# One encoder layer in float32 on one core: block stores and gate rows on GpSimd's queue, and the modulation's row sums behind the addition of each matrix' second bank

## The chip, the core and the metric

The kernel runs on one core of a Trainium2 chip. Its engines work side by side: TensorE multiplies matrices (PE, with weight loads as PEld), VectorE (DVE) and ScalarE (ACT) work element by element, GpSimd (POOL) and SyncE (SP) here do little but issue DMAs. Each engine runs its own instructions in order and waits on the others by semaphores. The metric is the device time of one execution, in microseconds (us).

## The reference, cut to what matters

```
h = x + 0.5 * g1 * postRMS(SwiGLU_1(mod1(preRMS(x))))      # FFN 1
h = h + g2 * postRMS(Mixer(mod2(preRMS(h))))               # two kinds of attention
h = h + 0.5 * g3 * postRMS(SwiGLU_2(mod3(preRMS(h))))      # FFN 2
swiglu(u, w_gate, w_up, w_down) = (silu(u @ w_gate) * (u @ w_up)) @ w_down
```

x is 1024 x 1024 in float32, D_FF is 2816. The shifts, scales and gates (mod1 to mod3, g1 to g3) are 9 columns of 1024 numbers: silu(c) times a 1024 x 9216 matrix, plus a bias.

## The kernel before, in words

Every product is computed as three float32r products of high and low halves, hence two operands "H" and "L" of everything (tiles wsH/wsL for weights) and three matmuls per 128 x 128 by 128 x 512 block, on lines 307 to 309.

The gate and up products of an FFN, the stage this is about, run over 11 pairs (NPAIR) of one gate and one up matrix, each a column block of 256 of the weights. An object `Matrix` forms its product by a Strassen-like scheme with seven block products of 12 matmuls instead of eight. TensorE's order within a matrix is: A11 and A12 times the input's first half (`start`), then `p6` (operand T2), `p5` (T1), `p7` (T3), `p3` (B22) and `p4` (T4); a pair is 168 matmuls. The products p7 and p4 pile up in one bank of PSUM with the former ones. After p7 VectorE adds this bank to the tile c22: that is `self.added`, L419. p4's first matmul writes into the same bank and so waits until L419 has read it. p3's addition is L424, and the first product's is L389.

The sums of weight blocks that the scheme needs (S1 to S4) come from two loads, raw (L325) and raw2 (L337) of 512 KB, and are four VectorE additions into two tiles s21 and s34: L340, L341, L351, L352. They are cast to H by ScalarE and to L by VectorE (L350, L232). A pair's two results give the hidden block silu(gate) x up; `hidden` (L488 to L491) forms its sums s21 and s34, and stores three blocks hd_A of 256 KB (L494) and two d_S of 512 KB to DRAM. `down_sums` does the like for the down weights (t21 and t34, L515 to L518) and stores two d_T of 512 KB. `both` issues the d_S and d_T stores on L505; `store_queue(c)` gives their queue, SP for all pairs but the last, POOL (GpSimd) for that. All of the tiles s21, s34, t21, t34 share one tag "s" of four buffers: a new sum waits until the store that reads the old tile has landed.

The modulation's columns are made beside all this. A row of the matrix (512 KB, tile wada) is loaded by SP, and one VectorE instruction multiplies it by silu(c) and sums it (`mod_sum`, L79: a custom instruction over 128 x 1024 and a read of its accumulator). 32 such row sums are steps of a generator in FFN 1 (eight for the gate g1, sixteen for mod2, eight for g2) and eight in FFN 2 (g3); `per_pair` says how many steps are taken after which pair: in FFN 1 none before pair 3, five after pairs 3 to 8, four after pair 9; in FFN 2 two from pair 2 on. A finished gate of eight columns goes to DRAM as a row (`g_dram`, L121), to be read back across all partitions.

The order of instructions on each engine is not written out: a scheduler takes the program's order, dependences and its own estimates, and moves an instruction ahead of others where its inputs are ready. `tc.issue_after(ins)` keeps what is issued in its block behind `ins`, on the same engine; no semaphore is added by it there. DMA issue is in the order of each queue.

Of the kernel before, what the change touches and what calls it, by code (L numbers as in the profile page):

```python
# [20 lines left out]
P = 128  # L21
D = 1024
S = 1024
NK = D // P
# [9 lines left out]
NPAIR = NFF // 2  # L34
# [12 lines left out]
def build(ctx, tc, A, out):  # L47
    nc = tc.nc
    V, ACT, PE, POOL, SP = nc.vector, nc.scalar, nc.tensor, nc.gpsimd, nc.sync
# [31 lines left out]
    def mod_col(mp, j, c, add, scale=None):  # L81

        t = const.tile([P, NK], F32, name=f"modcol{j}")
        for k in range(NK):
            w = mp.tile([P, D], F32, name="wada", tag="row", bufs=ROWS - 1)
            SP.dma_start(w, A["wada"][j * NK + k])
            mod_sum(w, c, t[:, k:k + 1], add[:, k:k + 1], 1.0 if scale is None else scale[:, k:k + 1])
            yield
        return t
# [4 lines left out]
    def post_cols(i):  # L94
        return badaT[:, (3 * i + 2) * NK:(3 * i + 3) * NK], npostT[:, i * NK:(i + 1) * NK]
# [21 lines left out]
    def mod_gate(mp, i, c):  # L117

        g = yield from mod_col(mp, 3 * i + 2, c, *post_cols(i))
        row = dram.tile([1, D], F32, name=f"g_dram{i}")  # L120
        SP.dma_start(row.rearrange("o (k p) -> p (o k)", p=P), g)  # L121
        gates[i] = row.broadcast_to([P, D])

    ab, gates = {}, {}
# [186 lines left out]
    class Matrix:  # L311
# [80 lines left out]
        second = "pb", 1  # L392
# [10 lines left out]
        def start(self):  # L403
            self.part(8)
# [30 lines left out]
    def rest(late, m, between=None):  # L435

        m.sums(late, False)
        m.sums34()
        m.last()
        if between is not None:  # L440
            between()
        m.p6()
        m.p5()
        m.p7()
        m.p3()
        m.p4()

    def rest_first(late, ms, done):

        for m in ms[:2]:
            m.p6()
        for i, m in enumerate(ms[:2]):
            m.p5()
            m.last()
            if i:
                ms[2].sums(late, True)
            m.p3()
            m.p7()  # L460
        for m in ms[:2]:
            m.p4()
        ms[2].sums34()
        ms[2].last()
        for i in range(2, len(ms)):
            m, nxt = ms[i], ms[i + 1] if i + 1 < len(ms) else None
            m.p6()
            done(i - 1)
            m.p5()
            m.p7()  # L470
            if nxt is not None:
                with tc.issue_after(m.copied.ins), tc.issue_after(m.added.ins):
                    nxt.sums(late, True)
            m.p3()
            if nxt is not None:
                nxt.sums34()
            m.p4()
            if nxt is not None:
                nxt.last()
        done(len(ms) - 1)  # L480

    def hidden(late, c, hs, hd):


        a11, a12, a21, a22 = hs["C11"], hs["C21"], hs["C12"], hs["C22"]
        s21 = late.tile([P, 2, HALF], F32, name="s21", tag="s", bufs=4)
        s34 = late.tile([P, 2, HALF], F32, name="s34", tag="s", bufs=4)
        V.tensor_add(s21[:, 1], a21, a22)  # L488
        V.tensor_sub(s21[:, 0], s21[:, 1], a11)
        V.tensor_sub(s34[:, 0], a11, a21)  # L490
        V.tensor_sub(s34[:, 1], a12, s21[:, 0])  # L491
        for n, t in (("A11", a11), ("A12", a12), ("A22", a22)):
            hd[n, c] = dram.tile([P, HALF], F32, name=f"hd_{n}_{c}_{len(hd)}")
            store_queue(c).dma_start(hd[n, c], t)  # L494
        both(hd, "S2", "S1", c, s21)
        both(hd, "S3", "S4", c, s34)

    def store_queue(c):

        return POOL if c == NPAIR - 1 else SP  # L500

    def both(hd, n0, n1, c, t):
        d = dram.tile([P, 2, HALF], F32, name=f"d_{n0}_{c}")
        hd[n0, c], hd[n1, c] = d[:, 0], d[:, 1]
        store_queue(c).dma_start(d, t)  # L505

    def down_sums(fp, late, src, c, hd):

        r1 = wpool.tile([P, 2, HALF], F32, name="raw", tag="raw", bufs=2)
        SP.dma_start(r1, src[:, 0:2])  # L510
        r2 = fp.tile([P, 2, HALF], F32, name="raw2", tag="raw2", bufs=2)
        SP.dma_start(r2, src[:, 2:4])
        t21 = late.tile([P, 2, HALF], F32, name="t21", tag="s", bufs=4)
        t34 = late.tile([P, 2, HALF], F32, name="t34", tag="s", bufs=4)
        V.tensor_sub(t21[:, 1], r1[:, 1], r1[:, 0])  # L515
        V.tensor_sub(t21[:, 0], r2[:, 1], t21[:, 1])
        V.tensor_sub(t34[:, 0], r2[:, 1], r1[:, 1])
        V.tensor_sub(t34[:, 1], r2[:, 0], t21[:, 0])  # L518
        both(hd, "T2", "T1", c, t21)
        both(hd, "T3", "T4", c, t34)  # L520

    def ffn(wg, wu, wd, start, pending, steps_fn, per_pair, steps2_fn, i, res_src, dst):


        hd = {}

        with tc.tile_pool(name="ffa", bufs=1, side="left", reuse_waits="tile") as fp, \
                tc.tile_pool(name="ffa_ps", bufs=1, space=PSUM, reuse_waits="tile") as psum:
            mats = {}

            def pair(c):
                g = Matrix(fp, psum, A[wg][c], None)
                mats[c] = g, Matrix(fp, psum, A[wu][c], g)
                return mats[c]

            first = [m for c in range(NFIRST) for m in pair(c)]
            start(fp, psum, first)
            with tc.tile_pool(name="fft", bufs=1, side="left", reuse_waits="tile") as tp, ExitStack() as more:
                pools = [tp]
                later = pending(pools, fp, psum, tag="y")  # L540
                for n, m in enumerate(first):
                    m.start()
                    if n:
                        next(later)
                with tc.tile_pool(name="ffs", bufs=1, side="left", reuse_waits="tile") as sp:
                    for m in first[:2]:
                        m.sums(sp, True, "s0")
                    for m in first[:2]:
                        m.sums34()
                pools.append(more.enter_context(tc.tile_pool(name="fft2", bufs=1, side="left", reuse_waits="tile")))  # L550
                for _ in later:
                    pass
                yp.close()
                with tc.tile_pool(name="late", bufs=1, side="right", reuse_waits="tile") as late:
                    steps = steps_fn(late)
                    def follow(n):
                        if n % 2 and n // 2 < NFIRST - 1:
                            hidden(late, n // 2, mats[n // 2][1].c, hd)
                        if n > 1:

                            if n % 2 == 0:
                                down_sums(fp, late, A[wd][n // 2 - 1], n // 2 - 1, hd)
                            for _ in range((per_pair(n // 2) + n % 2) // 2):
                                next(steps, None)

                    rest_first(late, first, follow)
                    for c in range(NFIRST, NPAIR):
                        for second, m in enumerate(pair(c)):
                            if second:
                                down_sums(fp, late, A[wd][c], c, hd)  # L570
                            m.start()

                            def between(m=m, c=c):
                                with tc.issue_after(m.summed.ins):
                                    hidden(late, c - 1, mats[c - 1][1].c, hd)
                                    if c == NFIRST + 1:
                                        down_sums(fp, late, A[wd][NFIRST - 1], NFIRST - 1, hd)

                            rest(late, m, None if second else between)
                        for _ in range(per_pair(c)):  # L580
                            next(steps, None)
                    hidden(late, NPAIR - 1, mats[NPAIR - 1][1].c, hd)
                    for _ in steps:
                        pass

        open_y()
        with tc.tile_pool(name="ffb0", bufs=1, side="left", reuse_waits="tile") as np_, \
# [9 lines left out]
            steps = steps2_fn(np_)  # L597
# [4 lines left out]
            def raw(n, c, cols=slice(0, HALF)):  # L602
                t = fp.tile([P, HALF], F32, name="stg", tag="stg", bufs=STG)[:, cols]
                loads.append(SP.dma_start(t, (A[wd][c][:, B[n]] if n in B else hd[n, c])[:, cols]))
                return t
# [57 lines left out]
            for p, (sn, tn, bk) in enumerate((("A11", "B11", "A"), ("A12", "B21", "B"), ("S2", "T2", "A"), ("S1", "T1", "B"),  # L663
# [8 lines left out]
                if p < 6:  # L672
                    for c in range(NPAIR):
# [5 lines left out]
                        with ahead:  # L679
                            s, t = halves(fp, raw(sn, c), "sb", SB), halves(fp, raw(tn, c), "tb", NPAIR)  # L680
# [820 lines left out]
```

## Time and the profile before

| | us |
|---|---|
| median of three runs | 2202.57 |
| the three runs | 2201.4, 2202.57, 2205.51 |
| the profiled execution | 2207.76 |
| its span | 2206.0 |
| TensorE busy | 2141.8 |
| VectorE busy | 1555.9 |
| ScalarE busy | 1050.0 |
| GpSimd busy | 58.4 |

The granted clock of TensorE was 0.994 of full speed over the span. FFN 1's gate and up products run from about 0 to 476 us, those of FFN 2 from about 1560 to 1980 us. In a row of the profile, "L419 TENSOR_TENSOR q<-bank,q 128x512" is an instruction of line 419 that writes tile q from tiles bank and q; "SPq" and "POOLq" are the DMA issues of the two queues; a bracket such as "[1.42 <-DVE q L419]" is how long the engine had been idle before, and what released it.

### The profile page before, as it was taken

Reading aid. Unit: us, or ns where it says so; the run is one execution under the profiler, and the core shown is the slowest. Engines: PE = TensorE matmul, PEld = TensorE weight load, DVE = VectorE, ACT = ScalarE, POOL = GpSimd, SP = SyncE. Lnnn points to the kernel's source line nnn. Section 1 sums busy time; section 2 is a strip of 40 time slices with the busy share of each in tenths; the row PEclk is TensorE's granted clock in tenths of the full one; section 3 lists DMA queues with packets and bytes.
Section 4 is the critical chain, followed back from the end, with each engine's and each line's share of the span. In section 5 each row is a group of like instructions: output and inputs, shape, how many; then the busy total and the mean of one; then the engine's idle time right before and its main releaser. Section 6 shows DMA issues by size and latency. Waiting matters only on the chain.

```text
span 2206.0 us, 28418 instructions
## 1 busy us (share of the span) xinstructions
PE 2141.8 (97%) x10328; PEld 1773.2 (80%) x10328; DVE 1555.9 (71%) x2629; ACT 1050.0 (48%) x1876; POOL 58.4 (3%) x84
## 2 busy tenths in 40 slices
PE   6899999999999999999999999999999999999997
PEld 4677788878887877888888988788788888888886
DVE  7989766658677678576677576665987767655566
ACT  6633333335465556455455455565733333334453
POOL 0000000000000010001011000000000000000000
PEclk9999999999999999999999999999999999999999
DMA  8488744359785111110212122763475644437675
GB/s 330 139 280 305 212 148 176 134 188 332 255 273 167 41 46 46 34 56 27 70 56 65 37 89 95 253 199 127 150 234 197 220 146 157 159 126 256 196 243 182
DMA packets 139791, 355.50 MB, mean 161 GB/s; under 512 B 19457, under 2 KB 29313, under 8 KB 139650
## 3 DMA queue, kind: packets, MB, share of 16 engines
q1 hardware_dynamic: 138018, 347.91, 46.5%
q0 software_dynamic: 1632, 5.77, 0.7%
q8 instruction: 81, 1.33, 0.2%
q14 instruction: 60, 0.49, 0.1%
HBM read 265.00 MB, written 88.62 MB: 160 GB/s over the span
## 4 chain that ended last, share of the span: by engine, by line
PE 76%; DVE 12%; DMA 6%; ACT 3%; issue 2%; SPq 0%; DVEq 0%; ACTq 0%
PE bank L307 10%; PE bank L308 10%; PE bank L309 10%; PE bankB L611 7%; PE bankA L611 7%; PE pps L940 5%; PE pps L942 5%; PE pps L944 5%; DMA stg<-d_T 2%; DVE f L1146 1%; PE vps L940 1%; PE vps L944 1%; PE vps L942 1%; PE pav L1157 1%; PE ops L193 1%
## 5 line engine op out<-in xcount | busy, mean ns | idle before, releaser
L940 PE MATMUL pps<-uH,wsH 128*128 128x512 f32 x512 | 209.7, 410 | 0.0
L942 PE MATMUL pps<-uL,wsH 128*128 128x512 f32 x512 | 204.8, 400 | 0.0
L944 PE MATMUL pps<-uH,wsL 128*128 128x512 f32 x512 | 203.5, 397 | 0.0
L232 DVE TENSOR_TENSOR tbL<-stg,tbH 128x512 fp32r<-128x512 f32 x154 | 106.0, 690 | 104.3 <-ACT tbH L231 103.9
L231 ACT CAST tbH<-stg 128x512 fp32r<-128x512 f32 x154 | 95.6, 621 | 148.1 <-DMA stg<-d_T 106.3
L307 PE MATMUL bank<-uH,wsH 128*128 128x512 f32 x352 | 138.4, 399 | 4.1 <-DVE q L389 1.6
L611 PE MATMUL bankA<-tbL,sbH 128*128 128x512 f32 x352 | 138.4, 393 | 3.8 <-DVE tbL L232 3.7
L308 PE MATMUL bank<-uL,wsH 128*128 128x512 f32 x352 | 139.4, 396 | 1.6 <-DVE uL L847 1.5
L309 PE MATMUL bank<-uH,wsL 128*128 128x512 f32 x352 | 139.0, 395 | 1.5 <-DVE wsL L232 1.5
L611 PE MATMUL bankA<-tbH,sbH 128*128 128x512 f32 x352 | 135.3, 394 | 4.8 <-DVE q L371 1.7
L611 PE MATMUL bankA<-tbH,sbL 128*128 128x512 f32 x352 | 137.4, 391 | 0.9 <-DVE sbL L232 0.9
L134 DVE TENSOR_TENSOR wsL<-raw,wsH 128x1024 fp32r<-128x1024 f32 x72 | 88.0, 1222 | 63.8 <-ACT wsH L134 59.4
L232 DVE TENSOR_TENSOR sbL<-stg,sbH 128x512 fp32r<-128x512 f32 (+1 forms) x176 | 108.2, 620 | 23.5 <-ACT sbH L231 22.7
L231 ACT CAST wsH<-raw 128x1024 fp32r<-128x1024 f32 (+1 forms) x88 | 73.5, 835 | 103.7 <-PE bank L308 85.1
L231 ACT CAST sbH<-stg 128x512 fp32r<-128x512 f32 (+1 forms) x176 | 98.2, 565 | 50.2 <-DMA stg<-hd_A 34.0
L944 PEld LDWEIGHTS pps<-uH,wsL 128*128 128x128 f32 x512 | 96.9, 189 | 17.8
L940 PEld LDWEIGHTS pps<-uH,wsH 128*128 128x128 f32 x512 | 97.7, 191 | 14.9
L942 PEld LDWEIGHTS pps<-uL,wsH 128*128 128x128 f32 x512 | 97.3, 190 | 14.3
L134 ACT CAST wsH<-raw 128x1024 fp32r<-128x1024 f32 x72 | 75.2, 1049 | 65.4 <-PE pps L942 36.5
L611 PE MATMUL bankB<-tbH,sbH 128*128 128x512 f32 x264 | 102.7, 389 | 0.0
L611 PE MATMUL bankB<-tbL,sbH 128*128 128x512 f32 x264 | 102.7, 389 | 0.0
L611 PE MATMUL bankB<-tbH,sbL 128*128 128x512 f32 x264 | 102.7, 389 | 0.0
(252 smaller groups left out, 5812.9 us busy)
## 6 DMA issues: line engine op xcount, KB each, us to landing
wada<-in_wada SPq DMA_DIRECT2D x56, 512.0 KB, 5.5
raw<-in_wg SPq DMA_DIRECT2D x50, 512.0 KB, 7.0
raw<-in_wu SPq DMA_DIRECT2D x50, 512.0 KB, 4.7
raw<-in_wd SPq DMA_DIRECT2D x44, 512.0 KB, 4.4
stg<-d_S SPq DMA_DIRECT2D x88, 256.0 KB, 3.7
stg<-d_T SPq DMA_DIRECT2D x88, 256.0 KB, 3.9
d_S<-s SPq DMA_DIRECT2D x40, 512.0 KB, 5.3
d_T<-t SPq DMA_DIRECT2D x40, 512.0 KB, 5.3
```

The lines of the kernel that those rows point to most:

```text
L134: made[:] = ACT.copy(h, raw).ins, eng.tensor_sub(l, raw, h.bitcast(F32)).ins
L193: PE.matmul(ps, aH, bL, start=False, stop=False)
L231: ACT.copy(h, src)
L232: eng.tensor_sub(l, src, h.bitcast(F32))
L307: PE.matmul(ps, H[:, ks], bH, start=first and k == 0, stop=False, skip_group_check=not first)
L308: PE.matmul(ps, H[:, ks], bL, start=False, stop=False, skip_group_check=not first)
L309: PE.matmul(ps, L[:, ks], bH, start=False, stop=k == 3, skip_group_check=not first)
L611: PE.matmul(ps, a[:, ts], b, start=first and n == 0, stop=last and n == 2, skip_group_check=not check)
L940: PE.matmul(ps, aH, bH, start=i == 0, stop=False)
L942: PE.matmul(ps, aH, bL, start=False, stop=False)
L944: PE.matmul(ps, aL, bH, start=False, stop=i == n - 1)
L1146: V.tensor_tensor_scan(fr, fr, fr, 1.0, ALU.mult, ALU.bypass)
```

## The change

```diff
@@ mod_gate
         row = dram.tile([1, D], F32, name=f"g_dram{i}")
-        SP.dma_start(row.rearrange("o (k p) -> p (o k)", p=P), g)
+        dst = row.rearrange("o (k p) -> p (o k)", p=P)
+        for k in range(0, NK, 4):
+            POOL.dma_start(dst[:, k:k + 4], g[:, k:k + 4])
         gates[i] = row.broadcast_to([P, D])
@@ hidden
-            store_queue(c).dma_start(hd[n, c], t)
+            POOL.dma_start(hd[n, c], t)
@@ both
-        store_queue(c).dma_start(d, t)
+        POOL.dma_start(d, t)
@@ ffn, in the loops over pairs and over a pair's two matrices
                             rest(late, m, None if second else between)
-                        for _ in range(per_pair(c)):
-                            next(steps, None)
+                            with tc.issue_after(m.added.ins):
+                                for _ in range((per_pair(c) + second) // 2):
+                                    next(steps, None)
```

(`store_queue` is deleted.) All block stores and the gate rows, each of these now two DMAs of four columns, are issued by GpSimd. The steps of the row sums, until now after a pair, come behind the addition `added` of each matrix: of five, two behind the gate matrix and three behind the up matrix. In FFN 1 that is in pairs 3 to 8, and two more behind each matrix of pair 9 as far as steps are left; in FFN 2, behind one matrix each, in pairs 3 to 5. Lines from L121 on stand two later in the changed program up to `hidden`, L505 is L503, and L515 to L518 are L513 to L516: L419 is now L421, and L340, L341, L351, L352 are L342, L343, L353, L354.

What this does to the order of VectorE's instructions in the steady part of FFN 2, first before. The row L419 is the addition of a gate matrix; s_17110 and s_17111 are the sums of the up matrix of its pair, s_17238 and s_17239 those of the next pair's gate matrix (whose tiles were t21 and t34 before).

```order
L340 TENSOR_TENSOR s_17110<-raw_17108 128x512
L341 TENSOR_TENSOR s_17110<-s_17110,raw 128x512
L351 TENSOR_TENSOR s_17111<-raw,raw_17108 128x512
L352 TENSOR_TENSOR s_17111<-raw,s_17110 128x512
L350 TENSOR_TENSOR wsL<-s_17110,wsH 128x512 x2
L419 TENSOR_TENSOR q<-bank,q 128x512
L340 TENSOR_TENSOR s_17238<-raw_17236 128x512
L351 TENSOR_TENSOR s_17239<-raw,raw_17236 128x512
L341 TENSOR_TENSOR s_17238<-s_17238,raw 128x512
L424 TENSOR_TENSOR q<-bank_17001,q 128x512
```

The same place in the changed program:

```order
L342 TENSOR_TENSOR s_17113<-raw_17111 128x512
L353 TENSOR_TENSOR s_17114<-raw,raw_17111 128x512
L343 TENSOR_TENSOR s_17113<-s_17113,raw 128x512
L354 TENSOR_TENSOR s_17114<-raw,s_17113 128x512
L342 TENSOR_TENSOR s_17241<-raw_17239 128x512
L353 TENSOR_TENSOR s_17242<-raw,raw_17239 128x512
L352 TENSOR_TENSOR wsL<-s_17113,wsH 128x512
L343 TENSOR_TENSOR s_17241<-s_17241,raw 128x512
L352 TENSOR_TENSOR wsL<-s_17113,wsH 128x512
L354 TENSOR_TENSOR s_17242<-raw,s_17241 128x512
L421 TENSOR_TENSOR q<-bank,q 128x512
L426 TENSOR_TENSOR q<-bank_17004,q 128x512
```

The four sums of the next pair's gate matrix stood behind the addition and now stand ahead of it, so the addition also waits for what they wait for. This is so at six gate matrices of FFN 2 (pairs 3 and 5 to 9) and at one of FFN 1 (pair 3).

VectorE in FFN 1, before, at the end of the blocks' sums of an early pair: s_1202 and s_1203 are sums of a hidden block, the L79 rows are row sums of the modulation, and L419 is the addition of the matrix then at work.

```order
L489 TENSOR_TENSOR s_1202<-s_1202,q 128x512
L79 ISA wada,modcol_2000<-wada,csil,colsT 128x1024
L79 ISA modcol_2000 128x1
L491 TENSOR_TENSOR s_1203<-q,s_1202 128x512
L79 ISA wada,modcol_2000<-wada,csil,colsT 128x1024
L79 ISA modcol_2000 128x1
L79 ISA wada,modcol_2000<-wada,csil,colsT 128x1024
L79 ISA modcol_2000 128x1
L419 TENSOR_TENSOR q<-bank,q 128x512
```

In the changed program, at the addition of the up matrix of FFN 1's pair 3 (L373 are the products of the up matrix' results with the gate's):

```order
L421 TENSOR_TENSOR q<-bank,q 128x512
L79 ISA wada,modcol_1530<-wada,csil,colsT 128x1024
L79 ISA modcol_1530 128x1
L373 TENSOR_TENSOR q<-q 128x512
L79 ISA wada,modcol_1530<-wada,csil,colsT 128x1024
L79 ISA modcol_1530 128x1
L426 TENSOR_TENSOR q<-bank_1623,q 128x512
L79 ISA wada,modcol_1530<-wada,csil,colsT 128x1024
L79 ISA modcol_1530 128x1
```

The row sums that stood ahead of the addition stand behind it, and with them between it and the next results.

GpSimd's queue, nearly empty before, in FFN 1 around the second half of a gate row (hd_A, d_S and d_T are the stores of hidden block and down weights, 48 to 50 and the like are numbers of blocks):

```order
L496 DMA hd_A_4_48_2072<-q 128x512
L123 DMA g_dram_1998<-modcol_1530 128x4x1
L496 DMA hd_A_4_50_2076<-q 128x512
L496 DMA hd_A_4_49_2074<-q 128x512
L503 DMA d_S_4_2078<-s_2066 128x1024
L503 DMA d_S_4_2080<-s_2067 128x1024
L503 DMA d_T_5_2169<-t_2163 128x1024
L503 DMA d_T_5_2171<-t_2164 128x1024
```

The stores of a pair now follow one another on this queue with the half rows among them. SP's queue, which had them all between the loads of weights, keeps the loads alone.

More of the change, by code (lines that the diff above doesn't have):

```diff
@@ L493, in hidden @@
             hd[n, c] = dram.tile([P, HALF], F32, name=f"hd_{n}_{c}_{len(hd)}")
-            store_queue(c).dma_start(hd[n, c], t)
+            POOL.dma_start(hd[n, c], t)
         both(hd, "S2", "S1", c, s21)
         both(hd, "S3", "S4", c, s34)
-    def store_queue(c):
-        return POOL if c == NPAIR - 1 else SP
     def both(hd, n0, n1, c, t):
```

## The prediction

> **What bounds the kernel now.** I read the page's head, the busy line and the chain first, then the stretches of the two gate/up stages, then the waits inside the one that is not full.
>
> ```profile
> span 2206.0 us, 28418 instructions
> PE 2141.8 (97%) x10328; PEld 1773.2 (80%) x10328; DVE 1555.9 (71%) x2629; ACT 1050.0 (48%) x1876; POOL 58.4 (3%) x84
> PE 76%; DVE 12%; DMA 6%; ACT 3%; issue 2%; SPq 0%; DVEq 0%; ACTq 0%
> ```
>
> TensorE is busy for 97% of the span, and the matmuls are not touched by the change: the number of them stays, and their order but for one swap. So the change can only take away or add time in which TensorE stands, and only in the gate and up products of the two FFNs, where its instructions are. Next the stretches (columns: window, its length, then busy time and count of PE, PEld, DVE, ACT and POOL, the granted clock, the DMA engines' share, GB/s):
>
> ```profile
> 120.00:150.00 30.00, 28.17 (x122) 22.30 (x121) 26.45 (x42) 9.63 (x15) 0.00 (x0) 1.00 0.75 263
> 150.00:180.00 30.00, 29.84 (x131) 24.05 (x129) 29.00 (x46) 12.88 (x19) 0.00 (x0) 1.00 0.90 321
> 180.00:210.00 30.00, 28.46 (x124) 22.92 (x123) 28.31 (x44) 9.95 (x16) 0.00 (x0) 1.00 0.83 276
> 210.00:240.00 30.00, 29.47 (x129) 23.75 (x129) 26.31 (x41) 10.53 (x16) 0.00 (x0) 1.00 0.87 313
> 240.00:270.00 30.00, 29.36 (x130) 23.83 (x129) 23.43 (x36) 9.79 (x16) 0.00 (x0) 1.00 0.76 178
> 270.00:300.00 30.00, 30.00 (x134) 24.86 (x133) 20.90 (x31) 10.65 (x17) 0.00 (x0) 1.00 0.52 183
> 1800.00:1830.00 30.00, 30.00 (x134) 24.86 (x133) 17.29 (x25) 10.49 (x16) 0.00 (x0) 1.00 0.31 112
> ```
>
> A full stretch holds 134 matmuls in 30 us (0.224 us each), at full clock. From 120 to 270 us, in FFN1, there are 636 where five full stretches would hold 670: 34 x 0.224 = **7.6 us lost**; by busy time 145.3 of 150, so 4.7 us, since a matmul's modelled end hides a part of each gap. From 270 us on, and in FFN2, the stage is full: nothing is to be won there, only lost. The waits of the weight loads in 120 to 270 us say at what TensorE stood, and the T4 group's row how much of that was idle time:
>
> ```profile
> PEld bank L307 <- DVE q L419: 5.7, 5, 1.8
> PEld bank L309 <- DVE wsL L350: 1.4, 2, 0.9
> PEld bank L309 <- DVE wsL L232: 1.0, 1, 1.0
> L307 PE MATMUL bank<-T4H,wsH 128*128 128x512 f32 x36 | 14.6, 406 | 3.5 <-DVE q L419 3.4
> ```
>
> The most costly is the first matmul of the seventh block product (T4). It writes over the bank that L419 must have read first, so it stands whenever VectorE comes late to L419. Why it is late is in VectorE's rows:
>
> ```profile
> L79 DVE CUSTOM_DVE_ANT_0 wada<-wada,csil,colsT 128x1024 f32<-128x1024 f32 x32 | 41.8, 1324 | 8.8 <-DMA wada<-in_wada 8.8
> ...
> 203.60 1.34 DVE L79 CUSTOM_DVE_ANT_0 wada<-wada,csil,colsT 128x1024 f32<-128x1024 f32 x1 [1.69 <-DMA wada<-in_wada]
> 204.87 0.68 DVE L419 TENSOR_TENSOR q<-bank,q 128x512 f32<-128x512 f32 x1
> ...
> 205.61 0.50 PE L307 MATMUL bank<-T4H,wsH 128*128 128x512 f32 x1 [1.42 <-DVE q L419]
> ```
>
> All 32 row sums of FFN1's modulation stand between 90 and 260 us, 1.32 us each, and VectorE is busy for 23 to 29 of each 30 us there against 21 after it. Here one sum waits 1.69 us for its row, runs 1.34, and only then L419 runs; 0.74 us after L419's start T4 goes. The last of the five stalls has another cause, a store that lands late:
>
> ```profile
> 261.71 0.69 DVE L351 TENSOR_TENSOR s<-raw,raw 128x512 f32<-128x512 f32 x1 [1.06 <-DMA d_S<-s]
> ...
> 264.87 0.50 PE L307 MATMUL bank<-T4H,wsH 128*128 128x512 f32 x1 [0.64 <-DVE q L419]
> ```
>
> **Term 1: the row sums go behind the addition.** The 32 sums move from 90 to 260 us into slots of two behind the gate matrix' addition and three behind the up matrix', in pairs 3 to 8, and two in pair 9. No sum can then stand ahead of the L419 of its own matrix, and the load is spread over six pairs of 38 us. VectorE has 30.00 - 20.90 = 9.1 us idle in 30 us without sums, 11.5 in a pair of 168 matmuls, 38 us; five sums are 5 x 1.32 = 6.6 us of it. Four of the five T4 stalls stand behind a sum: 3.4 us of idle time less the 0.64 at 264.87 is 2.8, say 3 us as the least gain. The most is all 7.6. The waits at wsL (L350, L232) are mostly VectorE running behind after such a stall, so they go with it, but a weight that comes late by itself stays. I take **-6.5 us**, near the upper end since the whole deficit lies in the stretch where the sums are.
>
> **Term 2: what stands behind the sums in FFN1.** Three sums behind the up matrix' addition are 3 x 1.32 = 4.0 us of VectorE time, into which the third product's addition and the hidden blocks' sums are queued; the d_S stores issue after those, and the next sums wait for these stores' landing. About 1.3 us of that time was idle, so this chain is 2.6 us later. At 261.71 the same wait has shown its price, 1.06 us with 0.64 us of it on TensorE. Six gate matrices can be so affected: 0 to 1.1 each, 0 to +7 in all. I take 0.3 each, **+2 us**, by the row at 264.87 halved, since the stores also no longer wait in SP's queue.
>
> **Term 3: the stores on GpSimd's queue, and the order that VectorE gets by it.** This is the term that I think decides. In the steady pair of before:
>
> ```profile
> 330.32 0.69 DVE L518 TENSOR_TENSOR t<-raw,t 128x512 f32<-128x512 f32 x1
> 338.64 0.69 DVE L419 TENSOR_TENSOR q<-bank,q 128x512 f32<-128x512 f32 x1 [0.55 <-PE bank L309]
> 339.43 0.69 DVE L340 TENSOR_TENSOR s<-raw 128x512 f32<-128x512 f32 x1
> 340.04 0.69 DVE L351 TENSOR_TENSOR s<-raw,raw 128x512 f32<-128x512 f32 x1
> ...
> 330.31 1.04 SPq L505 DMA_DIRECT2D d_T<-t  x2
> 332.44 1.13 SPq L337 DMA_DIRECT2D raw<-in_wg  x1
> ...
> 341.16 0.39 PE L307 MATMUL bank<-T4H,wsH 128*128 128x512 f32 x1
> ```
>
> L419 ends at 339.33, and only behind it come the next gate's sums (L340, L351), which need two things: the s tiles, free when the two d_T stores have landed, and the tile raw2, loaded at 332.44. T4 wants to start at 341.16, so L419 has until 341.16 - 0.74 = 340.4. In the changed order four sums of the next gate stand *ahead* of L419 (L421 there) at seven gates: six in FFN2 (pairs 3 and 5 to 9) and one in FFN1 (pair 3). From the start of the sum that needs the second d_T store to L421 are some five instructions at 0.6 us (339.43 to 340.04), 3.0 us; so that store must have landed by 340.4 - 3.0 = 337.4. VectorE ends the t tiles at 330.32 + 0.69 = 331.0; with half an issue of GpSimd's 0.62 us (1.25 for two, below) the store is out at 331.3, so it has **6.05 us from issue to landing**. The rows on that:
>
> ```profile
> 444.84 1.25 POOL L505 DMA_DIRECT2D d_T<-t  x2 [443.53 <-DVE t L516]
> ...
> d_T<-t POOLq DMA_DIRECT2D x2, 512.0 KB, 4.9
> ...
> d_T<-t POOLq DMA_DIRECT2D x2, 512.0 KB, 6.3
> stg<-hd_A SPq DMA_DIRECT2D x1, 256.0 KB, 6.3
> ...
> d_T<-t SPq DMA_DIRECT2D x2, 512.0 KB, 5.3
> raw<-in_wg SPq DMA_DIRECT2D x2, 512.0 KB, 6.9
> ```
>
> The first is how GpSimd issues a pair; the next two are its landings at 440 to 450 and 1943 to 1952 us, with 256 KB of another load beside the second; the last two are SP's at 326 to 333 us. On one queue the stores go first and the gate's loads behind them (6.9 us). With stores on a second queue the two loads, 1 MB, run beside them. Were the rate shared evenly, I estimate from 4.9 us with little beside and 6.3 with a quarter of that beside, some 7.2 us at the worst: 1.15 us late. The same holds for raw2, which landed at about 332.44 + 6.9 = 339.3 and is now wanted by about 337. Against that, the loads no longer wait for the stores' issue. So 0 to 1.1 us for each of the six gates of FFN2, 0 to +6.6, where nothing is to be won. I take 0.3 each, **+2 us**: the landing of 6.3 us is 0.25 late. The cover is the 0.25 to 1.2 us between a landing of 4.9 and of 6.05; with it gone, each further microsecond costs one per gate.
>
> The Trainium skill has a rule on this, in "DMA: Bandwidth & Descriptors", section "Issuing engines are not separate DMA queues": transfers started by different engines run on the same 16 DMA engines and interleave, and a second issuing engine saves only the time of issuing. The trace agrees as far as it goes (4.9 us alone, 6.3 beside a load). By that rule alone the stores' move would win nothing and this term would be its upper half.
>
> The issue itself costs nothing: POOL is busy 58.4 us of 2206, and 0.6 us an issue for some 150 stores hides behind its idle time; SP's queue is 0% of the chain, so taking them off it gains nothing there either.
>
> **Term 4: the gate row** goes from one DMA to two of four columns, behind the sums on GpSimd's queue, where hidden stores stand next to them.
>
> ```profile
> g_dram<-modcol SPq DMA_DIRECT2D x3, 4.0 KB, 9.7
> ...
> 121.00:131.00 10.00, 10.00 (x46) 8.29 (x45) 9.06 (x15) 5.11 (x9) 0.00 (x0) 1.00 0.35 27
> 132.00:142.00 10.00, 8.17 (x33) 5.78 (x33) 8.40 (x14) 2.07 (x3) 0.00 (x0) 1.00 1.02 416
> ```
>
> For ten microseconds after such a row's issue the DMA engines move 27 GB/s, and at once after it 416, when TensorE stands. Two halves should hold the transfers up for about 5 us each, estimated by halving 9.7, at a place between pairs' stores. A store held up so costs up to 3 us (that landing 5 us later, less the 1 to 2 us of slack above); none, if it falls where no store is due. I take **0** (0 to +3), since a stall of this kind, in before, is already in the 7.6.
>
> **The sum**: -6.5 + 2 + 2 + 0 = -2.5 us. The profiled execution took 2207.76 us for its span of 2206.0, so 2205.3 by it; it is 5.2 us above the median of the runs, 2202.57, and from that median I get **2200 us**. A measurement of this kernel tells some 0.2%, or 4.4 us, from no change.
>
> **The rivals.** *Faster*: the stores land in time everywhere, so terms 2 and 3 are nothing, and term 1 comes whole or with more: -6.5 to -7.6, 2195 to 2196. For it: POOL's landing of 4.9, and the loads that are issued earlier. Against it: the DMA engines at 400 GB/s in the steady pair. *Slower*: the store's landing passes 6.05 us, since the loads of the next gate interleave with it; at 7.2 the seven gates lose 1.15 us each, 8, the six others of FFN1 1 us each by term 2, 6, less 6.5: +7.5, 2210. Its place is L421 behind the four sums, and the point from which it decides against the gain is a mean lateness above 0.5 us at 13 gates. Against it: SP's own 5.3. *The stores' move does nothing and only the sums count*, the order being harmless: -4 to -6.5, 2196 to 2198.5; on the border of the first. *The change doesn't do what it says*: the sums could still reach ahead of an addition, that of the following matrix; 2 behind the gate's and 3 behind the up's are 2.6 and 4.0 us, and matrices are 19 us apart, so hardly.
>
> By the skill's section "Queues, rings and completion order" of the same page each DMA engine goes round between the queues that have work, a packet at a time; that is the even sharing of the slower rival, and no row here shows it alone at this place.
>
> **How the numbers follow.** My forecast, within 0.2%: 0.38. Faster by more (the first rival, and the better half of the third): 0.36. Slower: 0.26. The likeliest case' own range is 2198.2 to 2207. For 8 in 10 I take 2195 (term 1 at 7.6 with nothing given back) to 2210 (the slower rival's price), and leave the ends beyond to both sides, since several of the latenesses would have to come together for more.
>
> **What would show it.** Term 1: no T4 wait for L421 behind L79 in FFN1, and 134 matmuls in each 30 us from 120 to 240. Term 2: waits of sums for d_S at gate matrices 4 to 9 of FFN1. Term 3: in FFN2, waits of L342 or L353 for d_T or raw2 and, behind them, of T4 for L421 at six gates; landings of d_T on GpSimd's queue under or over 6.05 us tell the rivals apart. Term 4: no stretch of 27 GB/s longer than 6 us. I am wrong if VectorE's order on the chip has the waits elsewhere, above all if hidden stores queue behind a gate row on GpSimd.

## The result, and the profile after

The changed kernel took 2271.3 us (median of six runs, 2262.08 to 2276.92) where the kernel before took 2207.1 beside it: the ratio is 1.0286, 95% interval 1.027 to 1.0302. It is slower by some 63 us, far outside the range of the prediction. The page of the profiled execution (span, busy time of each engine, and the row of the first T4 matmuls):

```profile
span 2262.3 us, 28547 instructions
PE 2156.2 (95%) x10328; PEld 1780.7 (79%) x10328; DVE 1553.1 (69%) x2629; ACT 1047.9 (46%) x1876; POOL 140.5 (6%) x230
L309 PE MATMUL bank<-T4H,wsH 128*128 128x512 f32 x176 | 73.2, 416 | 33.7 <-DVE q L421 33.7
```

VectorE and ScalarE are busy as before. The span is 56 us longer, and TensorE's account of it has three parts: it stands 33.7 us ahead of the first T4 matmul, where it stood 3.5 before; it stands 11.9 us in four waits for a copy by ScalarE (at 265.29, 433.37, 1755.18 and 1840.82); and with the same 10328 matmuls it is busy 14.4 us longer, 2156.2 in place of 2141.8. The stretches, with the columns of before (two of FFN 2 at the end, where before had 443 matmuls in each):

```profile
120.00:150.00 30.00, 30.00 (x134) 24.86 (x133) 22.94 (x37) 11.26 (x18) 3.24 (x6) 1.00 0.56 193
150.00:180.00 30.00, 30.00 (x134) 24.84 (x133) 25.39 (x38) 11.40 (x18) 4.31 (x8) 1.00 0.80 278
180.00:210.00 30.00, 27.93 (x123) 22.80 (x122) 22.14 (x34) 9.32 (x14) 2.40 (x4) 1.00 0.55 143
210.00:240.00 30.00, 27.07 (x112) 21.88 (x112) 21.45 (x33) 9.91 (x15) 3.76 (x7) 0.94 0.82 280
240.00:270.00 30.00, 25.86 (x108) 20.40 (x106) 21.41 (x33) 7.45 (x12) 3.98 (x7) 0.94 0.71 215
1700.00:1800.00 100.00, 93.67 (x399) 76.33 (x398) 66.98 (x100) 31.13 (x47) 12.05 (x22) 0.97 0.62 199
1800.00:1900.00 100.00, 86.78 (x371) 70.43 (x370) 58.69 (x85) 30.56 (x46) 8.31 (x15) 0.97 0.40 128
```

The two stretches from 120 to 180 us are now full, so something of term 1 came. From 180 us on FFN 1 is worse than before, and FFN 2, which was full, loses 44 and 72 matmuls in these two stretches. One stall of FFN 2 in VectorE's and TensorE's rows (L342, L343, L353 and L354 are the sums, L352 the L half of the weights, L421 the addition):

```profile
1885.56 0.69 DVE L353 TENSOR_TENSOR s<-raw,raw 128x512 f32<-128x512 f32 x1 [3.40 <-DMA d_S<-s]
1886.17 0.69 DVE L343 TENSOR_TENSOR s<-s,raw 128x512 f32<-128x512 f32 x1
1886.89 0.69 DVE L354 TENSOR_TENSOR s<-raw,s 128x512 f32<-128x512 f32 x1
1888.50 0.69 DVE L342 TENSOR_TENSOR s<-raw 128x512 f32<-128x512 f32 x1 [0.92 <-DMA raw<-in_wg]
1889.52 0.69 DVE L353 TENSOR_TENSOR s<-raw,raw 128x512 f32<-128x512 f32 x1 [0.32 <-DMA d_T<-t]
1890.13 0.68 DVE L352 TENSOR_TENSOR wsL<-s,wsH 128x512 fp32r<-128x512 f32 x1
1890.73 0.69 DVE L343 TENSOR_TENSOR s<-s,raw 128x512 f32<-128x512 f32 x1
1891.33 0.69 DVE L352 TENSOR_TENSOR wsL<-s,wsH 128x512 fp32r<-128x512 f32 x1
1891.93 0.69 DVE L354 TENSOR_TENSOR s<-raw,s 128x512 f32<-128x512 f32 x1
1892.53 0.69 DVE L421 TENSOR_TENSOR q<-bank,q 128x512 f32<-128x512 f32 x1
...
1893.28 0.50 PE L309 MATMUL bank<-T4H,wsH 128*128 128x512 f32 x1 [3.27 <-DVE q L421]
```

Three waits for transfers stand ahead of the addition, one behind the other: 3.40 us for a d_S store, 0.92 for the next gate's load, 0.32 for a d_T store. The last one to end decides: when d_T has landed, at 1889.5, VectorE has five instructions left before the addition, 3.0 us. The last four sums, which stood behind the addition before, take from 1888.50 to 1892.53. T4 comes 3.27 us late. The transfers issued at this place (median us from issue to landing at the end):

```profile
d_S<-s POOLq DMA_DIRECT2D x2, 512.0 KB, 6.5
raw<-in_wg SPq DMA_DIRECT2D x2, 512.0 KB, 8.0
d_T<-t POOLq DMA_DIRECT2D x2, 512.0 KB, 9.0
```

9.0 us for d_T, where it took 5.3 on SP's queue, and the gate's loads are not earlier either.

### The profile page after: what moved, and what is told of

It is laid out like the page before. It is cut to its first block, busy times and chain, and to the rows that moved or that the text cites. A ratio compares the mean times of both kernels' runs of the same rounds, so it can differ in the third digit from the quotient of the medians.

```text
span 2262.3 us, 28547 instructions
## 1 busy us (share of the span) xinstructions
PE 2156.2 (95%) x10328; PEld 1780.7 (79%) x10328; DVE 1553.1 (69%) x2629; ACT 1047.9 (46%) x1876; POOL 140.5 (6%) x230
## 4 chain that ended last, share of the span: by engine, by line
issue 42%; PE 36%; DVE 8%; DMA 7%; POOL 3%; ACT 3%; SPq 0%; POOLq 0%; DVEq 0%; ACTq 0%
PE bankA L610 5%; PE bankB L610 5%; PE pps L939 4%; PE pps L941 4%; PE pps L943 4%; DMA stg<-d_T 3%; PE bank L309 2%; PE bank L311 2%; PE bank L310 2%; DMA stg<-in_wd 1%; DVE f L1145 1%; PE vps L939 1%; PE vps L943 1%; PE vps L941 1%; PE pav L1156 1%
## 5 line engine op out<-in xcount | busy, mean ns | idle before, releaser
L309 PE MATMUL bank<-T4H,wsH 128*128 128x512 f32 x176 | 73.2, 416 | 33.7 <-DVE q L421 33.7
```

The costliest lines, as they stand in the source:

```text
L309: PE.matmul(ps, H[:, ks], bH, start=first and k == 0, stop=False, skip_group_check=not first)
```

## The experiments

All ran beside the kernel before on the same chip. The first four take the change apart.

**The stores alone.** `store_queue` returns POOL for every pair; nothing else.

```diff
     def store_queue(c):
-        return POOL if c == NPAIR - 1 else SP
+        return POOL
```

> The kernel before with one part of the change: all block stores (hd_A, d_S, d_T) on GpSimd's queue; row sums and gate rows as before. Theory A (the stores' move is the loss: they go beside the next gate matrix' loads, land after 8 to 9.4 us in place of 5.4, and the additions behind them come late): 2250 to 2275 us, d_S and d_T landing at 8 us or more in FFN2, T4 waiting for L419 for some 40 us in all. Theory C (the row sums, 3 behind the up matrix' addition, make the loss): 2200 to 2210. Theory D (the gate rows hold GpSimd's queue up): 2200 to 2210.

Measured: 2272.01 us, ratio 1.0285 (1.0269 to 1.03). The stores alone make as large a loss as the whole change; theories C and D are not needed for its size.

**The row sums alone**, as in the diff of the change.

> The kernel before with the row sums alone moved behind the additions; stores and gate rows on SP. Theory A, with my term 1: 2195 to 2203, no T4 wait behind a row sum in 120 to 270 us. Theory C: 2220 to 2270, with sums in FFN1 waiting for d_S stores that were issued late.

Measured: 2211.89, ratio 1.0016 (1.0006 to 1.0027). Neither as expected. The stretch from 120 to 210 us is full, but there is one large new stall, and its rows (of VectorE, ScalarE and TensorE, and the window ahead of it) show where the gain went:

```profile
259.08 0.69 DVE L340 TENSOR_TENSOR s<-raw 128x512 f32<-128x512 f32 x1 [8.19 <-DMA d_S<-s]
...
259.88 0.62 ACT L346 CAST wsH<-s 128x512 fp32r<-128x512 f32 x1 [9.98 <-DVE s L340]
260.41 0.58 ACT L415 COPY q<-bank 128x512 f32<-128x512 f32 x1
...
261.04 0.80 PE L307 MATMUL bank<-B22H,wsH 128*128 128x512 f32 x1 [6.33 <-ACT q L415]
...
238.00:249.00 11.00, 11.00 (x50) 9.12 (x49) 10.96 (x18) 3.87 (x5) 0.00 (x0) 1.00 0.23 20
```

The gate row is issued at 237.7, right behind its last row sum, and from 238 to 249 us the DMA engines move 20 GB/s. The d_S stores fall into that; a sum waits 8.19 us for them, ScalarE waits for that sum, and the copy (L415) that TensorE needs is queued behind it: 6.33 us.

**The gate rows alone**, two halves on GpSimd's queue.

> The kernel before with the gate rows alone as two halves on GpSimd's queue. Theory A: within 3 us of before (my term 4: 0 to +3). Theory D: 2215 or more.

Measured: 2213.56, ratio 1.0019 (1.001 to 1.0029): some 4 us, a little more than theory A's bound.

**The change with its stores on SP.**

```diff
-            POOL.dma_start(hd[n, c], t)
+            store_queue(c).dma_start(hd[n, c], t)
...
-        POOL.dma_start(d, t)
+        store_queue(c).dma_start(d, t)
```

> The whole change except the block stores, which go back to SP (to GpSimd in the last pair alone). Theory A: 2195 to 2203, like the row sums alone, d_S and d_T landing in 5 to 6 us; theories C and D: still above 2240.

Measured: 2223.98, ratio 1.0073 (1.0054 to 1.0092). No theory had this. The row sums and the gate rows cost 0.2% each alone and 0.7% together: the sums' new place puts each half row beside the stores. So there are two losses, and the next runs took them one at a time.

**The stores alone, with VectorE's order held.** The next gate's sums are kept behind the gate's addition.

```diff
-    def rest(late, m, between=None):
-        m.sums(late, False)
+    def rest(late, m, between=None, behind=None):
+        with ExitStack() as order:
+            if behind is not None:
+                order.enter_context(tc.issue_after(behind.ins))
+            m.sums(late, False)
...
-                            rest(late, m, None if second else between)
+                            rest(late, m, None if second else between, mats[c - 1][0].added if c > NFIRST and not second else None)
```

> The stores alone on GpSimd's queue, and the next pair's gate sums held behind the gate matrix' addition, as they stood before the change (four sums, 2.4 us, no longer ahead of L419). Theory A1 (the late landing of d_S is enough: the up matrix' sums, which stood ahead of the addition in the kernel before too, wait for it): d_S still lands at 8 us, VectorE's waits for it stay, and 2235 us or more. Theory B (VectorE's order is the loss, the landing would be hidden by the order of before): 2205 to 2220 with the landings still at 8 us.

Measured: 2217.61, ratio 1.004 (1.0026 to 1.0054), where the same stores without the pin gave 1.0285. Theory A1, which was mine, fell: the landings are as late as with the stores alone (8.7 us for d_T and 5.2 for d_S there; first two rows, and the third row is the run with loads behind, below), and FFN 2 is full again from 1800 to 1900 us (this run, then the stores alone):

```profile
d_T<-t POOLq DMA_DIRECT2D x22, 512.0 KB, 8.5
d_S<-s POOLq DMA_DIRECT2D x18, 512.0 KB, 5.2
```
```profile
d_T<-t POOLq DMA_DIRECT2D x22, 512.0 KB, 5.5
```
```profile
1800.00:1900.00 100.00, 100.00 (x442) 82.79 (x442) 66.74 (x97) 36.28 (x54) 10.23 (x19) 1.00 0.49 171
```
```profile
1800.00:1900.00 100.00, 90.80 (x375) 73.66 (x374) 58.60 (x84) 30.42 (x46) 7.55 (x14) 0.94 0.41 143
```

VectorE at a gate of the pinned run shows why:

```profile
1808.92 0.69 DVE L351 TENSOR_TENSOR s<-raw,raw 128x512 f32<-128x512 f32 x1 [1.78 <-DMA d_S<-s]
...
1810.86 1.28 DVE L350 TENSOR_TENSOR wsL<-s,wsH 128x512 fp32r<-128x512 f32 x2
1812.27 0.69 DVE L419 TENSOR_TENSOR q<-bank,q 128x512 f32<-128x512 f32 x1
...
1813.87 0.69 DVE L351 TENSOR_TENSOR s<-raw,raw 128x512 f32<-128x512 f32 x1 [0.31 <-DMA d_T<-t]
```

The up matrix' sums still wait 1.78 us for d_S, but the addition then runs at once, and TensorE's next T4 has no wait. The wait for d_T is still there, and stands behind the addition, where nothing is late by it.

**The stores alone, with the gate's loads behind them on the same queue.** The loads raw and raw2 of the gate matrices from pair 3 on are issued by POOL.

```diff
-                SP.dma_start(raw, src)
+                self.queue.dma_start(raw, src)
...
-            SP.dma_start(r2, self.src[:, 2:4])
+            self.queue.dma_start(r2, self.src[:, 2:4])
...
+                            if not second:
+                                m.queue = POOL
```

> The stores alone on GpSimd's queue, and the gate matrices' weight loads of pairs 3 to 10 on the same queue, so that they are again in one line with the stores. Theory A2 (a store lands late since another queue's loads take turns with it): d_S and d_T land in 5 to 6.5 us and the time comes back to 2205 to 2225. Theory E (GpSimd's queue is slow by itself): landings of 8 us or more remain, 2245 or more.

Measured: 2215.62, ratio 1.0032 (1.002 to 1.0043); d_T lands in 5.5 us (above), as on SP. So GpSimd's queue is not slow: the store lands late because another queue's loads run beside it. The scheduler put none of the gate's four sums ahead of the addition here, so the time says nothing against theory B.

**One kind of store back on SP**, with hd_A and the other kind on GpSimd. (In `both`, a queue is given for d_S, or for d_T.)

> The stores alone on GpSimd's queue, but the two d_S stores back on SP, ahead of the gate's loads; hd_A and d_T stay on GpSimd. Theory A1: d_S lands in 5 to 6 us, the up matrix' sums are in time, most of the loss goes: 2205 to 2230. If d_T's landing, which my prediction named, decides: 2240 or more.

Measured: 2257.6, ratio 1.0216 (1.0198 to 1.0234). So d_S's late landing does not decide: with d_S in time the result is on the side that the expectation gave to d_T. Not all of it is d_T's, though, for I had not foreseen two single stalls: TensorE stands 10.03 us at 144.53, where VectorE waits for a row of the modulation behind a gate row, and 8.61 us at 2021.88, where SP holds the last pair's d_S stores, which it did not before, ahead of the next stage's loads. VectorE has two of the next gate's sums ahead of the addition here, and at one such place it is the gate's load that lands last, after a wait of 2.83 us.

> The stores alone on GpSimd's queue, but the two d_T stores back on SP; hd_A and d_S stay on GpSimd. VectorE then has two of the next gate's four sums ahead of the addition. Theory B: a stall at each of those gates that is between none (pinned) and the 2.9 to 3.9 us of four sums, some 1 to 2 us, 2225 to 2250, though d_T lands in 5 to 6 us. If late landings of d_T alone decided: 2205 to 2215.

Measured: 2229.89, ratio 1.0102 (1.0087 to 1.0116), within theory B's range. Two of four sums are ahead, and the T4 waits of the gates in FFN 2 are between those of four and of none. The waits of the weight loads on the addition from 1640 to 1960 us (total, times, longest) are 8.4 us with two sums ahead, 16.8 with four and 0.5 with none:

```profile
PEld bank L307 <- DVE q L419: 8.4, 6, 1.7
```
```profile
PEld bank L307 <- DVE q L419: 16.8, 5, 3.9
```
```profile
PEld bank L307 <- DVE q L419: 0.5, 1, 0.5
```

**The row sums, with the gate row later.** Stores on SP, sums moved; the row is one DMA on SP again, issued behind the second load of a later gate matrix.

```diff
+                            if rows and not second and c in (6, 7, 10):
+                                with tc.issue_after(m.load2.ins):
+                                    rows.pop(0)()
                             with tc.issue_after(m.added.ins):
```

(`rows` holds the row's DMA from `mod_gate`; `load2` is the load of raw2.)

> The row sums moved behind the additions (stores on SP), and each gate row's DMA, still one of 1024 elements on SP, issued behind the next gate matrix' second load, where no store is due for some 20 us. Theory G (the gate row's DMA holds all transfers up for some 10 us, and the sums' new place put it right ahead of the d_S stores; that ate the gain): no stall of 4 us or more in FFN1, 2200 to 2206 beside 2210 of before, ratio 0.995 to 0.998. Rival (the sums' place by itself gives nothing): 2209 to 2213.

Measured: 2201.05, ratio 0.9963 (0.9951 to 0.9976). This version beats both kernels. The stretches that were short before:

```profile
150.00:180.00 30.00, 30.00 (x134) 24.86 (x133) 27.08 (x40) 12.36 (x19) 0.00 (x0) 1.00 0.79 280
180.00:210.00 30.00, 30.00 (x134) 24.85 (x133) 22.91 (x36) 9.55 (x14) 0.00 (x0) 1.00 0.51 170
210.00:240.00 30.00, 29.29 (x128) 23.62 (x127) 23.98 (x36) 11.11 (x17) 0.00 (x0) 1.00 0.76 270
240.00:270.00 30.00, 30.00 (x134) 24.75 (x133) 26.20 (x40) 10.91 (x17) 0.00 (x0) 1.00 0.90 229
```

**The whole change with the order held**, and then also with the gate rows later. The edits are those above.

> The whole change, with one thing more: the next pair's gate sums held behind the gate matrix' addition. Theory B (that order, met with later landings, is nearly the whole loss, and the gate rows near the stores are the next): the T4 waits in FFN2 go, the stalls of 4 us near the half gate rows stay: 2218 to 2235. If something else in the change, working together, makes the loss: 2245 or more.

Measured: 2231.41, ratio 1.0109 (1.0095 to 1.0123), within theory B's range.

> As the one before, and the gate rows as one DMA each on SP behind the next gate's second load, as in the run that won. Theories B and G: what is left is the row sums' gain, some -7, and the later landings of the stores on GpSimd's queue, up to +9: 2201 to 2212. If it comes out at or below 2203, the stores' queue is harmless once the order holds; at 2208 or more it still costs.

Measured: 2209.23, ratio 1.0001 (0.9989 to 1.0013): the stores' queue still costs, about what the sums win.

**Halves on SP.** As the change with its stores on SP, but the half rows too are issued by SP.

> The row sums moved and the gate rows as two halves each, as in the change, but issued by SP; all stores on SP. It stands between the row sums alone (a whole row on SP, 2212) and the change with its stores on SP (halves on GpSimd, 2224). Theory H (a half costs about as much as a whole row, and there are twice as many beside the stores): 2218 to 2228. Theory Q (GpSimd's queue makes the halves costly): 2207 to 2214.

Measured: 2231.5, ratio 1.0097 (1.0081 to 1.0114), a little above theory H's range: the halves cost, whichever queue has them. A whole row on SP lands in 9.7 us in the kernel before; the halves here, and those on GpSimd in the change with its stores on SP, land no sooner (first and last row). While one runs, the others are slow: from 204 to 215 us here (second row) the DMA engines are full and move 192 GB/s, and beside the second half, from 245 to 256 us, they move 20, as beside the whole row in the run of the row sums alone:

```profile
g_dram<-modcol SPq DMA_DIRECT2D x6, 2.0 KB, 11.1
...
204.00:215.00 11.00, 11.00 (x50) 9.12 (x49) 6.92 (x11) 2.40 (x4) 0.00 (x0) 1.00 1.03 192
```
```profile
g_dram<-modcol POOLq DMA_DIRECT2D x6, 2.0 KB, 10.9
```

## Why the prediction was wrong, by its own steps

The account by ratios, in thousandths of the time before: the sums win 3.7 (sums with late rows); the stores' later landing under the order of before costs some 4 (stores pinned), which together make the 0.1 of the change with order held and rows late; the gate rows beside the stores cost 10.8 (1.0109 against 1.0001); the order costs the remaining 17.7 (1.0286 against 1.0109). With 2207.1 us that is -8, +9, +24 and +39. This split holds for this way of taking the change apart: with the stores alone the order costs 24.5 (1.0285 against 1.004), and the sums and the gate rows then add nothing to the whole (1.0286).

- **Term 3 failed, by its price and not its place.** The rival "slower" named the mechanism: L421 behind four sums, a landing past 6.05 us, loads of the next gate running beside the store. What was mis-sized is the landing, 6.3 us as likely and 7.2 as the worst, and with it the price of a late gate, 0.3 us and 1.15 at most. At 1893.28 d_T took 9.0 us and T4 came 3.27 late. My 7.2 had no working shown: the two rows beside it, 4.9 us and 6.3 with 256 KB more, would have allowed for much more with 1 MB. The other waits there add nothing, since the 3.40 us for d_S and the 0.92 for the gate's load were over before d_T had landed. It is so at all six gates of FFN 2. The sum that needs d_T (L353) starts 3.0 us ahead of the addition, as the prediction had it, but behind the last t sum it starts later than the 6.4 us for which there was room (331.0 to 337.4):

  | T4 at, us | last t sum to L353 | less 6.4 | T4 stands |
  |---|---|---|---|
  | 1717.88 | 9.6 | 3.2 | 3.04 |
  | 1803.48 | 9.0 | 2.6 | 2.43 |
  | 1849.68 | 14.4 | 8.0 | 5.84 |
  | 1893.28 | 9.8 | 3.4 | 3.27 |
  | 1933.50 | 8.4 | 2.0 | 1.85 |
  | 1975.40 | 10.1 | 3.7 | 3.53 |

  That is 20 us in all, and but for the third gate, where TensorE had been held up before, each stall is the excess within 0.2 us. The gate's second load lands nearly as late, as the prediction feared for it: with d_T in time the sum could have started 0 to 0.5 us earlier.
- **Three gates of FFN 1 were in no term.** I had counted the gates with four sums ahead of the addition. At 311.64, 353.31 and 394.25 one sum, L342, stands ahead of it and waits 3.43, 2.88 and 3.33 us for the gate's load; T4 stands 3.09, 1.99 and 2.56 us.
- **The loss is of order and landing together.** The landing as late as ever, with the order of before, costs 0.4%; with the changed order 2.85%. Two sums ahead cost in between. The changed order with all transfers in one queue was not tried, since in these runs the scheduler took that order only with a second queue; so what the order would cost by itself stays open.
- **Term 4 failed**: 0 to +3 us foreseen, +24 measured. I had halved 9.7 us and put the halves where no store is due. A half takes as long as a whole one, and the sums' new place, behind the addition, is some 6 to 9 us ahead of the d_S stores (on GpSimd's queue 203.95 us against 210.45, and 245.02 against 253.27). Moved to another place, a whole row on SP leaves no stall near it.
- **Term 1 was right**, -6.5 foreseen and 0.37%, -8, measured once the gate rows were out of the way; in the change itself 120 to 180 us show it. (The gate row's own stall of before, which the prediction counted in its 7.6 us, went with it; the run does not part the two.) **Term 2** asked for +2: with stores on SP and rows late, no T4 stall is left in FFN 1, so it was 0.
- **A price left out of all terms.** Some long stalls are followed by slow matmuls: after the 5.84 us of one at 1849.68, ten ran at 0.43 us in place of 0.22, with the granted clock at half (two windows, then TensorE's rows):

```profile
1849.60:1853.90 4.30, 4.22 (x10) 3.39 (x11) 1.84 (x3) 2.10 (x3) 0.00 (x0) 0.50 0.00 0
...
1893.20:1896.00 2.80, 2.73 (x12) 2.27 (x13) 1.76 (x3) 2.10 (x3) 0.00 (x0) 1.00 0.00 0
```
```profile
1849.68 0.80 PE L309 MATMUL bank<-T4H,wsH 128*128 128x512 f32 x1 [5.84 <-DVE q L421]
1850.27 0.63 PE L310 MATMUL bank<-T4L,wsH 128*128 128x512 f32 x1
```

That is another 2 us for that stall. Over the whole execution I estimate some 14 us from the granted clocks, 0.994 over 2206.0 us before and 0.988 over 2262.3 now, which is what TensorE's busy time grew by: a quarter of the loss. With the stores alone TensorE was busy for 2168.7 us, with the order held for 2145.7, so that 23 of the 58 us between the spans of these two runs are of this kind; the price of the order above has it in it. The Trainium skill, "TensorE: Matmul & The Clock Gate", section "Part 1: The HAM clock gate", says that the clock falls to half after an idle window of about 3.4 us, and that the windows run freely, so that the same stall may or may not meet one. The trace agrees in part: the stall of 3.27 us at 1893.28 is followed by twelve matmuls in 2.8 us at the full clock (second window), and that of 3.04 us at 1717.88 by half of it (0.50 from 1717.40 to 1720.80). But the latter is shorter than such a window, so here a stall did not need to last that long. The rule of the Trainium skill that the prediction cited from "DMA: Bandwidth & Descriptors", section "Issuing engines are not separate DMA queues", that all queues run on the same 16 DMA engines, held: the move of the stores to a second queue won nothing in any run, and with the loads in the same queue d_T's landing came back from 8.5 to 5.5 us.

## What to carry to other kernels

Where a scheduler decides the order, a change of queue is also a change of order: look, on the engine that waits, at what now stands ahead of the instruction that the bounding engine needs, and at which of the awaited transfers lands last; waits that end earlier cost nothing more, but every instruction between that landing and the needed one does. Hold such an instruction's place explicitly before stores are moved to another queue. A DMA of many tiny elements is best placed by what stands behind it in the next ten microseconds, and splitting it gives two such stretches rather than two halves of one.

## What the runs showed of the hardware that was not expected

Half of a gate row, 512 elements of four bytes, took 10.9 to 11.1 us to land (medians), where the whole row took 9.7 in the kernel before and 12.4 in the run with late rows. Nor does a half leave more to the others: beside two halves of one run the DMA engines moved 192 and 20 GB/s, beside two whole rows 20 (row sums alone, 238 to 249 us) and 214 (late rows, 1791.4 to 1802 us); what decides between these no run shows. Stores of 512 KB that landed in 5.5 us with the gate's loads behind them in the same queue took 8.5 with the loads on a second one. And a stall of 5.84 us cost a third again by the slower clock behind it.
